# A hybrid layer with top-4-of-32 experts: the phase ahead of the experts written anew, and another order of the last weights

## The chip, the cores and the metric

The kernel runs on one core of one Trainium2 chip. The metric is device time in microseconds (us): 1152.71 us, the median of three runs (1152.39 to 1156.62). One further execution was taken under the profiler; its own time is 1153.48 us.

## The reference

One layer over 256 tokens of 1024 channels, in float32, with 256 context tokens beside them. Biases, norms' gains and the routing by blocks are cut here; `mod` gives six vectors of 1024, from c for the tokens and from c_ctx for the context.

```python
x = x + pos_embed_2d(L)
sh1, sc1, g1, sh2, sc2, g2 = split(silu(c) @ w_mod + b_mod)            # 1024 x 6144
u = rmsnorm(x, norm1_g) * (1 + sc1) + sh1                              # the same for ctx with c_ctx
xa, ga, xb, xc, xd = split(u @ w_in + b_in)                            # 1024 x 1536
ya = (rglru_forward(xa) + rglru_backward(xa)) * gelu(ga)               # 4 causal taps, 2 gates, a scan;
                                                                       # starts from the context's last state
yb = pool_mixer(xb)                                                    # means over 2/4/8/16 positions
yc = fourier_mixer(xc)                                                 # 2-D DFT, real part, linear map
yd = silu(layernorm(conv31(xd[:, :256] * sigmoid(xd[:, 256:])))) @ w_pw
x = x + g1 * (concat(ya, yb, yc, yd) @ w_out + b_out)                  # 1024 x 1024
h = rmsnorm(x, norm2_g) * (1 + sc2) + sh2
top_vals, top_idx = top_k(h @ w_router + b_router, 4); gates = softmax(top_vals)
# each token goes to its 4 experts of 32:
gu = xb @ w_gu[e] + b_gu[e]                                            # 1024 x 2048 per expert
act = (clip(gu[:, 1024:]) + 1) * swish(min(gu[:, :1024], 7))
x = x + g2 * sum(gate * (act @ w_down[e] + b_down[e]))                 # 1024 x 1024 per expert
out = rmsnorm(x, final_norm_g)
```

## The kernel before

All of it is one function, `tile_hybrid_moe`, with a schedule written out by hand: each engine does its instructions in the order of the code, and waits only for data and for buffers. PE is the matrix engine, DVE the VectorE, ACT the ScalarE, POOL the GpSimd, SP the engine that issues the loads. One buffer `B` in SBUF holds everything; its first 18 MB are 18 slots of 1 MB. `bank` is one of eight accumulators of 128 x 512 in PSUM.

**Ahead of the experts** the slots hold the inputs x and ctx, the pieces of `w_mod` and `w_in`, `w_out` and the transposed activations `UT`. PE multiplies silu(c) by `w_mod` in pieces: `gemv_a` (L223) for shift and scale of the first norm, `gemv` 8 to 23 (L250) for the other four vectors. `transposes` turns the normed tokens, `modulate` applies scale and shift to them, `proj` (L309 with 512 columns, L311 with 256) multiplies by `w_in`, one row tile k of 128 at a time and twelve column tiles n. Then come the mixers, their pieces set between one another by hand: `lru_conv` (L424, L426), `lru_gates`, `lru_tanh`, `lru_mid` (L444 to L446), the 31 taps of the conformer convolution for two tiles of channels (62 in all) in `taps_dve` (43 of them on VectorE, L474 to L478) and `taps_act` (19, multiplied on ScalarE and added on GpSimd, L489), closed by `taps_sum` (L492); GpSimd makes the window sums. `scale_out` multiplies rows of `w_out` by g1, `out_mm` (L508) multiplies with the tokens as the weights of PE and 512 columns of `w_out` as what moves, into banks 0 to 3. The vectors that are needed along the free axis are spread over the partitions by GpSimd's `partition_broadcast` (L583, L697, L706, L707 ahead of routing, and L853 to L862 behind it).

`residual` (its add for one half on GpSimd, L772) makes x and its square sums, `norm2` and `hidden` (L785 on GpSimd) the router's input H, `turn` (L793) its transpose, `logits` (L799) the router product, `choose` the top 4, `gates` the softmax. `reseed` (L808) puts x back into the four banks `Y` that collect the result.

**The experts.** An expert's weights are 12 chunks of 1 MB, eight of w_gate_up and four of w_down; all 32 make 402.7 MB. `load_chunk` puts chunk i into slot `RING[i % 18]`, so a chunk can be loaded only when the chunk 18 before it has been multiplied, and the first 18 when the work ahead of the experts has left the slots. All these loads stand in one queue of SP, in the order of the experts. An expert takes at most 64 tokens at once (`CAP`); one with more goes through `block` a second time. For expert e the loop does: `down(e - 1)` (L953), a branch on the count (L1030), `keep` (L980), `gate_up(e)` (L927), `pick` (L904) and `turn_rows` (L912) for the rows of the next expert, `swiglu`, `turn_act` (L945), and the adding of older experts' results to `Y` by `scatter_part` (L984). The last expert's gate and up are cut by four of these, its down runs in two halves of the columns (`down_half`, L966; `keep_half`, L970), and `scatter_half` (L975) adds it in four pieces; the final norm reads the banks `Y`.

## Time and profile before

| | |
|---|---|
| median of three runs | 1152.71 us |
| profiled execution, its own time | 1153.48 us |
| its span (first to last instruction) | 1151.7 us |
| PE busy with matmuls | 1044.3 us, 91% of the span |
| PE busy with loading weights (beside them) | 426.5 us |
| VectorE, ScalarE, GpSimd busy | 307.9, 138.9, 64.6 us |
| DMA over the span | 444.83 MB, 386 GB/s |
| mean granted clock of PE | 0.976 of full speed |

The span is what the trace shows; 1.8 us of the execution lie around it. A share of busy time is a mean over stages that differ, so the rows below are taken stage by stage: ahead of the experts, the expert loop, and the end. In the trace a float32 matmul shows as two instructions, and its count "x" counts both. Some matmul records can be missing.

### The profile page before, as it was taken

The page shows a single profiled execution, that of the slowest core. Times are in us where ns is not written, and L with a number is a line of the kernel's source. Part 1 is how long each engine was busy: PE and PEld are TensorE (multiplying, and loading weights), DVE is VectorE, ACT ScalarE, POOL GpSimd, SP SyncE. Part 2 cuts the span into 40 slices and gives each one's busy share as a digit, 9 for nine tenths or more (in the row PEclk, how much of TensorE's full clock was granted, in tenths as well). Part 3 has the DMA queues.
Part 4 walks back from the last instruction along what each step waited for, and adds up shares of the span by engine and source line. Part 5 has one row for each costly group of instructions (what it writes and reads, how often), then busy time and mean ns, then how long its engine had stood idle before and what let it go on. Part 6 is the DMA issues. An engine that isn't in the chain of part 4 may idle for free. (4 is left out here: it accounts for less than half of the span.)

```text
span 1151.7 us, 12157 instructions
## 1 busy us (share of the span) xinstructions
PE 1044.3 (91%) x4810; PEld 426.5 (37%) x4810; DVE 307.9 (27%) x542; ACT 138.9 (12%) x250; POOL 64.6 (6%) x100
## 2 busy tenths in 40 slices
PE   4998495999999998999999999999889999989996
PEld 2654242333333333333333334444333333333333
DVE  4669494111111211222211111211111111111112
ACT  4335222000000000010000000000000000000002
POOL 2123543000000000000000000000000000000000
PEclk9998798999999999999999999999999999999999
DMA  8977676899999998999999999999999999999993
GB/s 333 376 276 254 238 305 256 334 421 420 420 420 420 421 422 347 422 420 420 421 421 419 421 421 420 419 420 422 420 421 419 421 421 421 420 420 421 421 406 131
DMA packets 68269, 444.83 MB, mean 386 GB/s; under 512 B 7300, under 2 KB 8132, under 8 KB 17448
## 3 DMA queue, kind: packets, MB, share of 16 engines
q1 hardware_dynamic: 67912, 443.36, 94.1%
q8 instruction: 72, 1.18, 0.4%
q14 instruction: 29, 0.24, 0.1%
q0 software_dynamic: 256, 0.05, 0.0%
HBM read 442.34 MB, written 1.05 MB: 385 GB/s over the span
## 5 line engine op out<-in xcount | busy, mean ns | idle before, releaser
L927 PE MATMUL bank<-B 128*64 128x512 f32 x2112 | 475.6, 600 | 12.7 <-DMA B<-in_w_gu_dram 10.9
L927 PEld LDWEIGHTS bank<-B 128*64 128x64 f32 x2112 | 178.8, 138 | 287.8 <-issue 225.7
L953 PE MATMUL bank<-B 128*64 128x512 f32 x1024 | 226.0, 594 | 0.9 <-ACT B L946 0.4
L933 DVE TENSOR_SCALAR B<-bank 128x512 f32<-128x512 f32 x33 | 22.8, 692 | 465.7 <-issue 436.8
L953 PEld LDWEIGHTS bank<-B 128*64 128x64 f32 x1024 | 71.3, 137 | 135.5 <-issue 127.2
L934 ACT ACTIVATE B<-B 128x512 f32<-128x512 f32 x33 | 20.8, 632 | 750.3 <-DVE B L933 750.3
L980 DVE TENSOR_TENSOR B<-bank,B 64x512 f32<-64x512 f32 x64 | 44.1, 689 | 243.6 <-PE bank L953 242.9
L984 PE MATMUL bank<-B 128*128 128x512 f32 x136 | 69.9, 618 | 0.9 <-DVE B L980 0.9
L904 PE MATMUL bank<-B 128*64 128x512 f32 x264 | 66.9, 606 | 1.1 <-DVE B L886 1.1
L916 PE MATMUL bank<-T,E 96*64 96x512 bf16 x196 | 35.6, 395 | 28.4 <-PEq L1030 21.2
L1060 POOL MEMSET B<- 64x1024 f32 x1 | 0.9, 947 | 869.6 <-PE bank L984 869.6
L311 PE MATMUL bank<-B 128*128 128x256 f32 x160 | 38.6, 391 | 0.0
L916 PEld LDWEIGHTS <-E 96*64 96x64 bf16 x196 | 10.9, 106 | 70.3 <-issue 69.3
L904 PEld LDWEIGHTS bank<-B 128*64 128x64 f32 x264 | 22.4, 139 | 36.9 <-issue 33.8
L984 PEld LDWEIGHTS bank<-B 128*128 128x128 f32 x136 | 22.0, 190 | 37.6 <-issue 24.9
L311 PEld LDWEIGHTS bank<-B 128*128 128x128 f32 x160 | 30.2, 193 | 14.2 <-issue 10.6
L913 DVE COPY B<-bank 128x512 f32<-128x512 f32 x33 | 22.8, 692 | 43.8 <-PE bank L912 43.8
L508 PE MATMUL bank<-B 128*128 128x512 f32 x64 | 28.3, 597 | 0.4 <-DVE B L503 0.4
L908 ACT ACTIVATE B<-bank 128x512 f32<-128x512 f32 x33 | 19.7, 597 | 50.7 <-PE bank L904 50.7
L946 ACT ACTIVATE B<-bank 128x512 f32<-128x512 f32 x33 | 19.7, 597 | 48.8 <-PE bank L945 48.8
L912 PEld LDWEIGHTS bank<-B 128*128 128x128 f32 x132 | 16.1, 141 | 22.5 <-ACT B L908 20.6
L478 DVE SCALAR_TENSOR_TENSOR B<-B 128x256 f32<-128x256 f32 x41 | 23.9, 583 | 1.4
(276 smaller groups left out, 581.3 us busy)
## 6 DMA issues: line engine op xcount, KB each, us to landing
B<-in_w_gu_dram SPq DMA_DIRECT2D x256, 1024.0 KB, 19.8
B<-in_w_down_dram SPq DMA_DIRECT2D x127, 1024.0 KB, 19.8
B<-in_w_mod_dram SPq DMA_DIRECT2D x16, 1024.0 KB, 5.1
B<-in_w_mod_dram SPq DMA_DIRECT2D x16, 512.0 KB, 9.9
B<-in_w_in_dram SPq DMA_DIRECT2D x8, 768.0 KB, 13.1
B<-in_w_out_dram SPq DMA_DIRECT2D x4, 1024.0 KB, 6.7
B<-in_ctx_dram SPq DMA_DIRECT2D x1, 1024.0 KB, 5.5
B<-in_x_dram SPq DMA_DIRECT2D x1, 1024.0 KB, 7.6
```

The costliest lines, as they stand in the source:

```text
L311: pe.matmul(half(b, t), w, UT[:, k, 256:512], start=(k == 0 and t == 0), stop=(k == KT - 1 and t == 1))
L478: dve.scalar_tensor_tensor(dst, src, w, dst, op0=ALU.mult, op1=ALU.add)
L508: pe.matmul(bank[2 * c + q], YT[:, k, c * P:(c + 1) * P], w_out_k(k)[:, 512 * q:512 * q + 512], start=first, stop=last)
L904: pe.matmul(mis[0][64 * g:64 * g + 64, :], p[:, c, :], H[:, c, 512 * g:512 * g + 512], start=(c == 0), stop=(c == 1))
L913: dve.tensor_copy(dst, ps.rearrange("p (j n) -> p j n", j=4))
L916: pe.matmul(dst[64 * g:64 * g + 64, :], E3[:, e:e + 1].to_broadcast([96, CAP]), T[:, col:col + 512], start=True, stop=False)
L927: pe.matmul(dst[64 * g:64 * g + 64, :], xt[:, k % 4, (k // 4) * 64:(k // 4) * 64 + 64], w[:, b * 1024 + g * 512:b * 1024 + g * 512 + 512], ...
L933: dve.tensor_scalar(GH, G0, 7.0, 0.5, op0=ALU.min, op1=ALU.mult)
L934: act.activation(TH, GH, AF.Tanh, scale=1.702)
L953: pe.matmul(dst[64 * g:64 * g + 64, :], AT[:, k % 4, (k // 4) * 64:(k // 4) * 64 + 64], dn[e, k, g], start=False, stop=(k == KT - 1))
L980: dve.tensor_tensor(out=dst[p0:p0 + 64, 512 * g:512 * g + 512], in0=ps[64 * g:64 * g + 64, :], in1=G2B[64 * g:64 * g + 64, :], op=ALU.mult)
L984: pe.matmul(Y[c][q], s[:, c * P:(c + 1) * P], o[:, 512 * q:512 * q + 512], start=False, stop=False)
```

## The change

The phase between the loads and the first expert is written anew, and the last two experts' chunks come in another order.

- **Loads and start.** The identity comes as a load (no `make_identity`). `w_in` is loaded in two parts, `W_1` (columns of xa and xd) first and `W_2` later, in place of rows of 6 KB. The biases of the experts are split into three bf16 parts on 128 partitions, and 12 small copies on GpSimd's DMA queue spread them. All four of the first `gemv_a` stand ahead of the turning of x, and `turned_x` applies scale and shift while it empties the bank. The raw x is turned as well, into `XT`.
- **Mixers.** All 62 taps are VectorE's, over four sums. The mixers' order is new: first xa and xd, then xc, xb and ga.
- **Output projection.** `out_mm` has `w_out` as PE's weights and 256 tokens as what moves, so the result comes out transposed; g1 is applied per partition when `finish` adds it to `XT`. The broadcasts of g1, of the bias, of scale and shift ahead of routing go.
- **Routing.** The router multiplies `XT` by rows of `w_router` that were scaled by A2 (`A2c`), a row `LB` holds the bias; the norm's factor comes in behind the product. `natural` turns `XT` back, `seed` puts it into the banks `Y`. H is only scaled by the norm, so `turn_rows`, which runs for every expert, applies A2 and the shift in two VectorE instructions where one copy stood.
- **End.** The chunks come as gate and up of expert 30, gate and up of 31, down of 30, down of 31; `down(30)` stands behind `gate_up(31)`, and expert 30 has its second run, should it need one, in the loop behind the end.

```diff
-W_OUT = [10, 11, 12, 14]
-RING = [4, 0, 1, 2, 3, 13, 15, 8, 5, 6, 7, 9, 10, 11, 14, 12, 16, 17]
+W_OUT = [12, 14, 10, 11]
+RING = [1, 2, 3, 9, 13, 15, 0, 8, 4, 6, 5, 7, 10, 14, 11, 12, 17, 16]
...
+        def load_in1(k):
+            sp.dma_start(W_1[:, k, 0:256], w_in[k * P:(k + 1) * P, 0:256])
+            sp.dma_start(W_1[:, k, 256:768], w_in[k * P:(k + 1) * P, 1024:1536])
+        def load_in2(k):
+            sp.dma_start(W_2[:, k, :], w_in[k * P:(k + 1) * P, 256:1024])
...
+        def turned_x(k):
+            dve.tensor_scalar(UT[:, k, 256:512], half(3 + k // 2, k % 2), A1c[:, k:k + 1], S1c[:, k:k + 1],
+                              op0=ALU.mult, op1=ALU.add)
...
+        for j in range(3):
+            for b in range(4):
+                pool.dma_start(T[32 * j:32 * j + 32, 768 * b:768 * b + 768], BP[32 * b:32 * b + 32, j, :])
...
-        def taps_act(n):
...
-                    act.activation(tp, src, AF.Copy, scale=wdh[:, 2 * j + 1:2 * j + 2])
-                    pool.tensor_tensor(out=ACC[:, 1, :], in0=ACC[:, 1, :], in1=tp, op=ALU.add)
...
+        sums = {(0, 0): ACC[:, 0, :], (1, 0): ACC[:, 1, :], (0, 1): ACC3, (1, 1): ACC2}
+        turns = [(t, j) for j2 in range(0, NTAP, 2) for j in (j2, j2 + 1) if j < NTAP for t in range(2)]
...
+                src, dst, w = V[:, t, j:j + 256], sums[t, j % 2], wdh[:, 2 * j + t:2 * j + t + 1]
...
+                    dve.scalar_tensor_tensor(dst, src, w, dst, op0=ALU.mult, op1=ALU.add)
...
-        def out_mm(k, cs, first=False, last=False):
-            for c in cs:
-                for q in range(2):
-                    pe.matmul(bank[2 * c + q], YT[:, k, c * P:(c + 1) * P], w_out_k(k)[:, 512 * q:512 * q + 512],
-                              start=first, stop=last)
+        def out_mm(k, first=False):
+            for i in range(KT):
+                pe.matmul(half(i // 2, i % 2), w_out_k(k)[:, i * P:(i + 1) * P], YT[:, k, :],
+                          start=(first and i % 2 == 0), stop=False)
...
+        def finish(b):
...
+            for i in (2 * b, 2 * b + 1):
+                dve.scalar_tensor_tensor(XT[:, i, :], half(b, i % 2), G1c[:, i:i + 1], XT[:, i, :],
+                                         op0=ALU.mult, op1=ALU.add)
+        def natural(i):
+            for c in range(2):
+                pe.transpose(N[c][i // 4][:, (i % 4) * P:(i % 4 + 1) * P], XT[:, i, c * P:(c + 1) * P], ident)
+        def seed(c):
+            for i in range(KT):
+                pe.matmul(Y[c][i // 4][:, (i % 4) * P:(i % 4 + 1) * P], XT[:, i, c * P:(c + 1) * P], ident,
+                          start=(i % 4 == 0), stop=False)
+        def logits(k):
+            g = k % 4
+            pe.matmul(bank[0][32 * g:32 * g + 32, 0:256], WRT[:, k, :], XT[:, k, :], start=(k < 4), stop=(k >= 4))
...
+        rsqrt_newton(rs2, w2, tn2)
+        act.activation(SM[:, 1:2], epsc, AF.Exp)
+        for c in range(2):
+            dve.scalar_tensor_tensor(LG[:, c, :], LR[:, c, :], rs2[:, c:c + 1], LB, op0=ALU.mult, op1=ALU.add)
             for q in range(2):
+                act.activation(H[:, c, cols2[q]], N[c][q], AF.Copy, scale=rs2[:, c:c + 1])
...
         def turn_rows(dst, ps):
...
-            dve.tensor_copy(dst, ps.rearrange("p (j n) -> p j n", j=4))
+            dve.tensor_tensor(out=d4, in0=ps.rearrange("p (j g s) -> p j g s", j=4, g=2),
+                              in1=jg(A2c).unsqueeze(3).to_broadcast([P, 4, 2, CAP]), op=ALU.mult)
+            dve.tensor_tensor(out=d4, in0=d4, in1=jg(SH2c).unsqueeze(3).to_broadcast([P, 4, 2, CAP]), op=ALU.add)
...
+        stream = [(e, k) for e in range(NE - 2) for k in range(NCH)]
+        stream += [(e, k) for ks in (range(KT), range(KT, NCH)) for e in (NE - 2, NE - 1) for k in ks]
...
-        gate_up(e, XET, {4: rest[0:2], 5: rest[2:4], 6: rest[4:5]})
-        rest[5]()
+        gate_up(e, XET)
         swiglu()
-        turn_act(e)
+        down(e - 1, mis[1])
+        turn_act(e, AT2)
+        with tc.If(r > CAP):
+            block(e, CAP)
+        keep(OP[1], 0, mis[1])
         down_half(e, 0, range(KT))
         keep_half(0)
         down_half(e, 1, range(4))
+        scatter_part(SS[1], OP[1], 0, 0, 0, 480)
+        scatter_part(SS[1], OP[1], 1, 0, 0, 480)
         down_half(e, 1, range(4, KT))
-        scatter_half(0, ((0, 0, 256), (1, 0, 224)))
         keep_half(1)
```

What the order of instructions on an engine becomes is shown at three places, of before and of the change apart. The first is VectorE between the copy of the first projection (L511 before, L613 now) and the last tap. L424 and L426 (now L481, L483) are the four-tap convolutions, L444 to L446 (now L501 to L503) the middle of a gate, L474 to L478 (now L531 to L535) the 31 taps.

```order
L530 SCALAR_TENSOR_TENSOR B<-B 128x256 x2
L424 TENSOR_SCALAR B<-B 128x512
L426 SCALAR_TENSOR_TENSOR B<-B 128x512 x3
L444 SCALAR_TENSOR_TENSOR B<-B 128x512
L445 SCALAR_TENSOR_TENSOR B<-B 128x512
L446 SCALAR_TENSOR_TENSOR B<-B 128x512
L444 SCALAR_TENSOR_TENSOR B<-B 128x512
L445 SCALAR_TENSOR_TENSOR B<-B 128x512
L446 SCALAR_TENSOR_TENSOR B<-B 128x512
L474 TENSOR_SCALAR B<-B 128x256
L478 SCALAR_TENSOR_TENSOR B<-B 128x256 x7
```

```order
L531 TENSOR_SCALAR B<-B 128x256 x2
L533 TENSOR_SCALAR B<-B 128x256 x2
L535 SCALAR_TENSOR_TENSOR B<-B 128x256 x2
L501 SCALAR_TENSOR_TENSOR B<-B 128x512
L502 SCALAR_TENSOR_TENSOR B<-B 128x512
L503 SCALAR_TENSOR_TENSOR B<-B 128x512
L501 SCALAR_TENSOR_TENSOR B<-B 128x512
L502 SCALAR_TENSOR_TENSOR B<-B 128x512
L503 SCALAR_TENSOR_TENSOR B<-B 128x512
L535 SCALAR_TENSOR_TENSOR B<-B 128x256 x30
L656 TENSOR_TENSOR B<-bank_77,B 128x512
L535 SCALAR_TENSOR_TENSOR B<-B 128x256 x26
```

Six taps now stand ahead of the middles of the first two gates and 56 behind them without another gate between; before, the taps on VectorE come in groups of 8, 10, 13 and 12 with the other gates between.

The second is PE from the last product of the output projection that both have (the residual's banks are 70 to 73 before) to the first expert's bias. L793 turns the router's input before, L808 is the seeding before and `natural` now, L813 `seed`, L799 before and L818 now the router product, L904 and L912 (now L929, L937) pick and turn the first expert's rows; the LDWEIGHTS and their matmuls on UB and OB (the positions of the tokens) are cut at the "...".

```order
L808 MATMUL bank_70<-B 128x512
L808 MATMUL bank_71<-B 128x512
L793 MATMUL bank_74<-B 128x128 x4
L793 MATMUL bank_75<-B 128x128 x4
L799 MATMUL bank_76<-B 32x128 x8
L808 MATMUL bank_72<-B 128x512
L804 MATMUL bank_77<-B 128x32
...
L904 MATMUL bank_76<-B 64x512 x4
L912 MATMUL bank_77<-B 128x128 x4
L1026 TENSOR_LOAD CNT
```

```order
L818 MATMUL bank_70<-B 32x256 x4
L845 MATMUL bank_71<-B 128x32 x2
L813 MATMUL bank_72<-B 128x128 x4
L813 MATMUL bank_73<-B 128x128 x4
L871 LDWEIGHTS UB
...
L929 MATMUL bank_70<-B 64x512 x4
L937 MATMUL bank_71<-B 128x128 x4
L813 MATMUL bank_76<-B 128x128 x4
L813 MATMUL bank_77<-B 128x128 x4
L1055 TENSOR_LOAD CNT
```

The turning of H goes from the way to the router, and half of the seeding stands behind the turning of the first expert's rows.

The third is PE at the end: from the last products of gate and up of the last expert (L927, now L956; bank 75 is the up half's) to the last scattering before the count's branch. L897 turns gated one-hot columns, L953 (now L980) is a whole down product, L966 (now L993) a half one, L945 (now L972) the turning of the activations.

```order
L984 MATMUL bank_72<-B 128x512
L927 MATMUL bank_74<-B 64x512 x2
L927 MATMUL bank_75<-B 64x512 x2
L984 MATMUL bank_73<-B 128x512
L945 MATMUL bank_76<-B 128x128 x4
...
L966 MATMUL bank_77<-B 64x256 x16
...
L966 MATMUL bank_76<-B 64x256 x16
L975 MATMUL bank_70<-B 128x256
L975 MATMUL bank_70<-B 128x224
```

```order
L956 MATMUL bank_75<-B 64x512 x2
...
L980 MATMUL bank_71<-B 64x512 x16
L972 MATMUL bank_70<-B 128x128 x4
...
L993 MATMUL bank_71<-B 64x256 x16
...
L993 MATMUL bank_70<-B 64x256 x8
L1008 MATMUL bank_72<-B 128x480
L1008 MATMUL bank_76<-B 128x480
L993 MATMUL bank_70<-B 64x256 x8
```

The down product of the last expert but one now stands between the last gate and up and the two half products, and two scatterings stand inside the second half.

## Rows read from the trace of the kernel before

**Rows 1.** Windows: stretch, its us, five engines' busy us, clock, DMA, GB/s.
```profile
0.00:202.00 202.00, 151.72 (x706) 81.41 (x708) 132.10 (x263) 68.59 (x120) 63.26 (x97) 0.91 0.77 291
202.00:740.00 538.00, 524.36 (x2423) 203.82 (x2420) 103.75 (x161) 39.65 (x71) 0.00 (x0) 1.00 1.00 412
740.00:1102.00 362.00, 329.02 (x1480) 123.89 (x1478) 62.22 (x96) 23.57 (x42) 1.33 (x3) 0.99 1.01 420
```
The engines stand in the order PE, PEld, DVE, ACT, POOL, each with its instructions; then the granted clock, the DMA engines' busy share and the rate.

**Rows 2.** Windows of 1 us: where the DMA stands, and the last weights.
```profile
205.00:206.00 1.00, 1.00 (x5) 0.36 (x4) 0.00 (x0) 0.00 (x0) 0.00 (x0) 0.57 0.00 0
1133.00:1134.00 1.00, 1.00 (x12) 0.70 (x10) 0.00 (x0) 0.00 (x0) 0.00 (x0) 1.00 0.07 27
```

**Rows 3.** Timeline of PE: the last router product and the first expert matmul.
```profile
190.23 0.92 PE L799 MATMUL bank<-B 128*32 128x128 f32 x16 [0.25 <-ACT B L794]
...
201.91 0.62 PE L927 MATMUL bank<-B 128*64 128x512 f32 x2
```
A row has the start, the busy us, the engine, line and operation, what it writes and reads with the shape, the count, and in brackets the idle time before it with what ended it.

**Rows 4.** Waits of PE: who waits for whom, us, times, longest.
```profile
PE bank L619 <- DVE B L492: 15.5, 1, 15.5
...
PE bank L927 <- DMA B<-in_w_gu_dram: 10.9, 21, 0.6
PE bank L793 <- POOL B L785: 7.6, 1, 7.6
```

**Rows 5.** Timeline of GpSimd: the taps, and the residual's add.
```profile
127.71 6.36 POOL L489 TENSOR_TENSOR B<-B 128x256 f32<-128x256 f32 x8 [11.07 <-issue]
...
181.41 1.08 POOL L772 TENSOR_TENSOR B<-B 128x512 f32<-128x512 f32 x1 [7.85 <-issue]
```

**Rows 6.** Window: the first 23 us.
```profile
0.00:23.00 23.00, 9.36 (x45) 5.71 (x48) 9.74 (x24) 8.60 (x15) 6.24 (x22) 0.93 0.87 312
```

**Rows 7.** Timeline of PE ahead of the experts, one row of each kind.
```profile
28.55 1.93 PE L223 MATMUL bank<-B 128*32 128x256 f32 x32
...
32.65 1.98 PE L309 MATMUL bank<-B 128*128 128x512 f32 x4 [1.17 <-ACT B L242]
...
60.90 7.03 PE L309 MATMUL bank<-B 128*128 128x512 f32 x16
67.76 3.62 PE L311 MATMUL bank<-B 128*128 128x256 f32 x16
...
73.03 1.06 PE L250 MATMUL bank<-B 128*32 128x512 f32 x8
...
89.24 1.05 PE L548 MATMUL bank<-B 128*128 128x128 f32 x8
```

**Rows 8.** Timeline of VectorE: convolution, evictions, gated input, gates, taps.
```profile
68.55 2.33 DVE L426 SCALAR_TENSOR_TENSOR B<-B 128x512 f32<-128x512 f32 x3
...
78.18 0.88 DVE L528 TENSOR_SCALAR B<-bank,B 128x256 f32<-128x256 f32 x2 [1.67 <-PE bank L311]
79.48 0.79 DVE L530 SCALAR_TENSOR_TENSOR B<-B 128x256 f32<-128x256 f32 x2 [0.42 <-ACT B L524]
...
83.01 0.68 DVE L444 SCALAR_TENSOR_TENSOR B<-B 128x512 f32<-128x512 f32 x1
...
88.38 3.96 DVE L478 SCALAR_TENSOR_TENSOR B<-B 128x256 f32<-128x256 f32 x7
```

**Rows 9.** Timeline of the first norm's Newton chain.
```profile
24.12 0.17 DVE L193 TENSOR_SCALAR B<-B 128x2 f32<-128x2 f32 x1 [1.44 <-ACT B L192]
25.55 1.15 ACT L195 ACTIVATE B<-B 128x1024 f32<-128x1024 f32 x1 [1.02 <-DVE B L180]
```

**Rows 10.** Timeline of the end: last expert, its halves, the last scattering.
```profile
1109.93 8.78 PE L927 MATMUL bank<-B 128*64 128x512 f32 x40
...
1131.64 3.67 PE L966 MATMUL bank<-B 128*64 128x256 f32 x32 [0.52 <-ACT B L946]
...
1139.02 0.43 DVE L970 TENSOR_TENSOR B<-bank,B 128x256 f32<-128x256 f32 x1 [3.17 <-PE bank L966]
1141.66 2.41 PE L975 MATMUL bank<-B 128*128 128x32 f32 x12 [0.96 <-PEq L1082]
```

More of the change, by code (lines that the diff above doesn't have):

```diff
@@ new lines, in ln_var, with ln_scale, gemvs @@
+        def ln_var(t):
+            pe.matmul(half(ln_b[t], 0), ONE, hlf(SQ, t), start=True, stop=True)
+            act.activation(hlf(SQ, t), half(ln_b[t], 0), AF.Sqrt, bias=epsc)
+        def ln_scale(t):
+            dve.tensor_tensor(out=hlf(VC, t), in0=hlf(VC, t), in1=hlf(SQ, t), op=ALU.mult)
+            dve.tensor_scalar(hlf(VC, t), hlf(VC, t), lgh[:, t:t + 1], lgh[:, 2 + t:3 + t], op0=ALU.mult, op1=ALU.add)
+        def gemvs(*ks):
+            for i in ks:
+                gemv(i)
+        tiles(XA_, (4, 5, 6, 7))
@@ new lines, in tile_hybrid_moe @@
+        dve.tensor_scalar(xa_view(0), two(bank[0]), bin_(0), None, op0=ALU.add)
+        act.activation(xa_view(1), two(bank[1]), AF.Identity, bias=bin_(1))
+        tiles(DD, (4, 5, 6, 7))
+        load_mod(12)
+        load_out(2)
+        lru_conv((0, 1))
+        lru_gates(0)
+        gemvs(8, 9)
+        for t in range(2):
+            act.activation(VT[:, t, :], half(3, t), AF.Tanh, scale=0.5, bias=hb[:, t:t + 1])
+        lru_tanh(0)
+        for t in range(2):
+            dve.tensor_scalar(V[:, t, 15:271], half(2, t), bin_(8 + t), None, op0=ALU.add)
@@ new lines, in tile_hybrid_moe @@
+        for t in range(2):
+            dve.scalar_tensor_tensor(V[:, t, 15:271], VT[:, t, :], 1.0, V[:, t, 15:271], op0=ALU.add, op1=ALU.mult)
+        lru_gates(1)
+        lru_tanh(1)
+        lru_conv((2, 3))
+        tiles((6, 7), range(8))
+        for t in range(2):
+            act.activation(XC[:, 256 * t:256 * t + 256], half(5, t), AF.Identity, bias=bin_(6 + t))
+        gemvs(10, 11, 12)
+        for t in range(2):
+            for q in range(2):
+                pe.matmul(bank[4][:, 256 * t + 128 * q:256 * t + 128 * q + 128], CS[:, q, :], BD[:, 10 + t, :],
+                          start=(t == 0 and q == 0), stop=(t == 1 and q == 1))
@@ new lines, in tile_hybrid_moe @@
+        lru_gates(3)
+        lru_tanh(3)
+        taps(36)
+        gemvs(13, 14, 15)
+        dve.tensor_tensor(out=MB_, in0=bank[7], in1=MB_, op=ALU.add)
+        for t in range(2):
+            for q, M in enumerate((CL, SL)):
+                for c in range(2):
+                    pe.matmul(half(5, t), Z[:, c, t, 128 * q:128 * q + 128], M[:, c, :],
+                              start=(t == 0 and q == 0 and c == 0), stop=(t == 1 and q == 1 and c == 1))
+        for t in range(2):
+            act.activation(YT[:, 4 + t, :], half(5, t), AF.Identity, bias=v("bf", t))
@@ L753, in tile_hybrid_moe @@
+        Y = [[bank[2], bank[3]], [bank[6], bank[7]]]
         rt = R(O_RT, 572)
@@ L803, in rows_of @@
[L803 to L811 removed]
+        LR = bank[1][:, 0:64].rearrange("p (c e) -> p c e", c=2)
+        CN = bank[1][:, 128:160]
```

834 lines of the change are left out of this document (380 added, 454 removed).

## The prediction

> **What bounds the kernel now.** I read first the busy times of three long stretches [rows 1]. From 202 us on the DMA moves 412 and then 420 GB/s without a break: the experts' weights, 402.7 MB, come in as fast as this kernel ever loads anything. In the first 202 us it moves only 291 GB/s, though PE is busy for 151.7 of them: 202 x (420 - 291) / 420 = 62 us of transfer time are lost there. The reason is in the ring: 18 slots of 1 MB are full before the first expert multiplies, and no weight can be loaded until a slot is given back. The first expert matmul starts at 201.91 us [rows 3]; the DMA still stands at zero between 205 and 206 [rows 2] and runs from then on. At the other end it moves 27 GB/s on average between 1133 and 1134 [rows 2], the last of the weights: I put their landing at 1133.2.
>
> So the time is a sum: T0 (201.9), then 931.3 us of weight stream up to the last landing, then 18.5 us to the end of the span (1151.7), and 1.8 us around it (the profiled execution took 1153.48; the median of the three runs is 1152.71, 0.8 below). Between T0 and the last landing PE was the tighter of the two until about 740 us (524.4 busy of 538) and the DMA after that (PE 329.0 of 362) [rows 1]; in all PE waited only 10.9 us for weights [rows 4]. Both start at T0, so whatever T0 gains, both keep. That makes T0 the first question and the last 18.5 us the second.
>
> **T0, from the start.** The waits of PE [rows 4] name what is lost before T0: 15.5 us for taps that VectorE closes after GpSimd, 7.6 us for a GpSimd add of the router's input. Both stand behind an idle GpSimd: 11.07 us with no releaser before the taps go on, 7.85 us before the add [rows 5], each time just after a partition broadcast and an ISA row in the order. In the new order no broadcast lies ahead of routing, the taps are VectorE's, and no GpSimd work stands between the output projection and T0.
>
> What is left I take as PE's own work, since almost all of it is in one row on that engine. Its start: the first four w_mod tiles, with all that is loaded ahead of them, are 7.0 MB; at the 312 GB/s of the first 23 us [rows 6] they land at 22.4 us. Before, 4.1 us pass from the start of the last products with them (28.55) to the first projection (32.65) [rows 7]. Now VectorE applies scale and shift as it empties four halves of banks (0.44 each, from the 0.88 for two [rows 8]) and 8 transposes follow (0.13 each): 2.8 us more. First projection at 22.4 + 4.1 + 2.8 = 29.3.
>
> From there on, by the pitches of [rows 7] (x counts instructions in the trace, two for one f32 matmul): 48 of 512 columns at 0.44 = 21.1 (32 in the projections, 16 for the gates); 332 of 256 columns at 0.226 = 75.0 (64 + 96 in the projections, 128 in the transposed output projection, 44 in the mixers); 16 adaLN products at 1.06 = 17.0; the second four of the first kind, twice 1.93; the small Fourier product 1.05; 34 transposes at 0.13 = 4.5; the router products twice 0.92, for twice the columns [rows 3]. Sum 124.3. The output projection is no saving: 128 x 0.226 = 28.9 where 64 x 0.44 = 28.1 stood. I add 3 us for short waits in the last stage, where PE and VectorE take turns bank by bank, and get the last router product at 29.3 + 124.3 + 3 = 156.6.
>
> Before, that point is 191.15 (190.23 + 0.92), and T0 follows 10.8 us later [rows 3]. Now the norm is computed beside the router and not before it, so its chain comes after: one more ScalarE pass and the Newton chain (1.43 us from 24.12 to 25.55 [rows 9]), 2.5 in all; 0.4 because both halves of the tokens choose together; and the second seeding of the accumulators, 16 instructions of 128 columns at 0.13 = 2.1, stands on PE between the turning of the first expert's rows and its first matmul. T0 = 156.6 + 10.8 + 2.5 + 0.4 + 2.1 = 172.4, a gain of 29.5 us.
>
> **What has to stay beside it.** VectorE: the projection of the first mixer ends at 56 on PE (29.3 + 14.1, 7.2 for the first half of the fourth mixer's, 3.9 and 1.6 for transposes). Behind it stand in order the copy (0.7), 16 convolution passes (at most 2.33 / 3 = 0.78 each, 12.4), the gated input (0.88 + 0.79), the middle of two gates (6 passes of 0.68, 4.1), 62 taps and their sums (0.8), all by [rows 8], with 1 us of waits. The taps' price is the open one. Before, each tap adds to the result of the one in front: 7 in 3.96 us, 0.566. Two passes of that size that don't depend on each other take 0.79, 0.395. The new taps go round four sums, so I take 0.40: 24.8 us, and VectorE is done at about 101.5. PE comes to the first use (the mean) 49 us behind 56, at 105 (7.2 for the rest of the fourth mixer, 14.4 for two more pairs of column tiles, 7.0 for gates, 13 adaLN products, 6.5 for the Fourier mixer). With 0.566 it would be 35.1 us and 111.8, a wait of 6 to 7 us. The nearest row for a pass without a dependence is the 0.395, so the forecast has no wait; the range keeps both.
>
> [...]
>
> The DMA: 39.2 MB of other inputs and 17 slots of weights must be in by T0, 57.0 MB. The last loads of w_out wait until the last projection has left its slots (117 us by the list above); from there 3 of them and 14 weight tiles, 17.8 MB at 420 GB/s, need 42 us, until about 161. That is 11 us ahead of T0, so the ring is full again but for the slot that holds the residual stream (free with the seeding, less than 2 us before T0), and the weight stream restarts about 4 us behind T0 as before. The twelve small copies that spread the bias tables go out on GpSimd's queue and are needed only by the first expert.
>
> The expert loop: the turning of rows gets a second VectorE pass (about 0.7). PE does not need it before its next gate and up, and a whole down projection lies between. I count it at nothing; without that cover it is 0.7 for each expert, in the half where PE is the tighter (18 experts) 13 us.
>
> **The end.** Before, PE runs gate and up of the last expert from 1109.93 with the scattering of two older experts cut in between, and reaches the down halves at 1131.64, one after the other, 3.67 each, by [rows 10]. Now all gate and up tiles come before the last two downs, so PE does the interleaved work while the down tiles come in. After the last landing there remain half of the second half (1.8), 1 us that PE is behind by then, two evictions at 0.43 (one before), and the 2.2 us from there to the final scattering at 1141.66 with the 10.0 us after it, unchanged: with small gaps 16.2 where 18.5 stood. Gain 2.3. The bounds: 5 if nothing is behind, a loss of 3 if the down of the last but one is.
>
> Sum: 1153.48 - 29.5 - 2.3 = 1121.7 for a profiled execution, 1121 beside the median.
>
> **Rivals.** (1) VectorE is late: taps at 0.566, PE waits 6 us before the means. For it: all the taps that the trace shows ran at that pace; against it: they were dependent. T0 179, time 1127. (2) The DMA is late: it is not the full ring but the loads that decide. For it: loads of w_out stand on one queue ahead of 14 weight tiles. It decides from 11 us of delay on; with 20 us the time is 1130. (3) PE is quicker: no short waits, 0.44 for every pair of 256-column instructions as for one of 512, and the end gains 5. T0 166, time 1112; from 162 on the DMA limits it. (4) Slower: w_in now comes in lines of 1, 2 and 3 KB in place of 6 KB, and PE cannot pass a product whose tile is missing. If the 6.3 MB took 15 + 32 = 47 us, 134 GB/s, all the gain is gone; at 100 GB/s T0 is 221 and the time 1169. Against it: w_mod in 1 KB lines is in the 312 GB/s of the first 23 us. (5) The extra pass of the loop is uncovered: 1134.
>
> **Numbers.** Forecast as summed, 1121, its own range 1115 to 1126: 0.55. Rival (1) 0.17, (2) 0.08, (3) 0.10, (5) 0.05, (4) and the like 0.05. All but the last are faster by over 0.5% (under 1147), which is about what a measurement of this kernel can tell from no change. Faster 0.93, the same 0.03, slower 0.04. Range 1108 to 1136: it leaves out the far ends of (2) and (4) and a quicker PE than (3).
>
> **What would show it.** In the new profile the first expert matmul near 173 us and no PE idle of over 3 us between 30 and 145; VectorE's last tap before PE's mean product; no GpSimd idle row ahead of routing that anyone waits for; DMA at zero for some microseconds just before T0; the stretch from T0 to the last landing still near 931 us; the last landing some 16 us before the end. A first matmul later than 182, or a DMA that never stops before T0, would prove the sum wrong.

## The result and the profile after

The changed kernel takes 1121.12 us (median of 4 runs, 1118.96 to 1123.31) where the kernel before takes 1152.55: ratio 0.9733, 95% interval 0.971 to 0.9755. In a second set of runs it was 1120.24 us, ratio 0.9718 (0.9687 to 0.9749). Forecast were 1121 and a range of 1108 to 1136. The profiled execution took 1123.31 us with a span of 1121.4.

The three long stretches of the changed kernel, cut at its own first expert matmul, in the columns of [rows 1]:

```profile
0.00:172.00 172.00, 149.05 (x798) 100.62 (x799) 107.04 (x277) 59.13 (x111) 34.85 (x77) 0.93 0.89 339
172.00:660.00 488.00, 476.46 (x2214) 182.27 (x2214) 105.80 (x163) 35.70 (x64) 0.00 (x0) 1.00 1.00 412
660.00:1072.00 412.00, 374.71 (x1689) 126.83 (x1688) 81.85 (x124) 27.45 (x49) 0.00 (x0) 1.00 1.01 420
```

The first stretch is 30 us shorter with nearly the same PE work (149.0 us busy in place of 151.7): what went is idle time. Behind it the rates are the 412 and 420 GB/s of before, and GpSimd does nothing at all.

PE's timeline at the points on which the sum was built:

```profile
34.53 1.88 PE L378 MATMUL bank<-B 128*128 128x512 f32 x4
...
60.12 7.07 PE L380 MATMUL bank<-B 128*128 128x256 f32 x32
67.03 1.88 PE L489 MATMUL bank<-B 128*128 128x512 f32 x4
...
101.75 4.50 PE L293 MATMUL bank<-B 128*32 128x512 f32 x40
106.17 1.13 PE L595 MATMUL bank<-B 128*128 128x256 f32 x4
...
157.00 0.64 PE L818 MATMUL bank<-B 128*32 128x256 f32 x8
...
168.10 3.62 PE L813 MATMUL bank<-B 128*128 128x128 f32 x16
172.02 0.62 PE L945 MATMUL bank<-T,E 96*64 96x512 bf16 x4 [0.30 <-PEq L1060]
172.45 13.93 PE L956 MATMUL bank<-B 128*64 128x512 f32 x64
```

The first projection is at 34.53, the means at 106.17 without a wait, the last router product ends at 157.64, the first expert matmul is at 172.45 (201.91 in [rows 3]). VectorE's taps end ahead of the means:

```profile
78.90 11.96 DVE L535 SCALAR_TENSOR_TENSOR B<-B 128x256 f32<-128x256 f32 x30
...
102.22 0.76 DVE L539 TENSOR_TENSOR B<-B 128x256 f32<-128x256 f32 x2
```

The stretches in which the DMA stops, restarts and ends (answering to [rows 2]):

```profile
160.00:163.00 3.00, 1.02 (x11) 0.70 (x10) 2.16 (x15) 2.99 (x6) 0.00 (x0) 1.00 0.83 347
...
166.00:168.00 2.00, 1.31 (x6) 0.81 (x5) 0.00 (x0) 0.60 (x1) 0.00 (x0) 0.50 0.00 0
...
174.00:175.00 1.00, 1.00 (x6) 0.33 (x4) 0.00 (x0) 0.00 (x0) 0.00 (x0) 1.00 0.97 410
...
1104.00:1105.00 1.00, 1.00 (x14) 0.61 (x10) 0.00 (x0) 0.00 (x0) 0.00 (x0) 1.00 0.37 143
1105.00:1106.00 1.00, 1.00 (x6) 0.49 (x3) 0.00 (x0) 0.00 (x0) 0.00 (x0) 1.00 0.06 20
```

The ring is full from about 163 (161 was forecast), and the loads run at their full rate again from 174, 1.5 us behind the first expert matmul, where the prediction had 4. In windows of 0.2 us the DMA falls to nothing at 1105.6; read in the same way, it did so at 1133.6 before, a little behind the 1133.2 of the prediction. From the first expert matmul to there it is 933.1 us (931.7 before), from there to the end 15.8 (18.1 before). So 29.5 us came from the front and 2.3 from the end, and the stream between gave 1.4 back.

### The profile page after: what moved, and what is told of

The parts are those of the page before. It is cut to its first block, busy times and chain, and to the rows that moved or that the text cites. A ratio compares the mean times of both kernels' runs of the same rounds, so it can differ in the third digit from the quotient of the medians.

```text
span 1121.4 us, 12287 instructions
## 1 busy us (share of the span) xinstructions
PE 1036.5 (92%) x4888; PEld 424.1 (38%) x4888; DVE 305.3 (27%) x588; ACT 128.7 (11%) x239; POOL 34.9 (3%) x77
## 5 line engine op out<-in xcount | busy, mean ns | idle before, releaser
L956 PE MATMUL bank<-B 128*64 128x512 f32 x2112 | 473.4, 596 | 35.4 <-DMA B<-in_w_gu_dram 34.1
L956 PEld LDWEIGHTS bank<-B 128*64 128x64 f32 x2112 | 160.4, 137 | 329.1 <-issue 224.2
L980 PE MATMUL bank<-B 128*64 128x512 f32 x1024 | 228.2, 598 | 2.7 <-DMA B<-in_w_down_dram 1.8
L960 DVE TENSOR_SCALAR B<-bank 128x512 f32<-128x512 f32 x33 | 22.8, 692 | 464.3 <-issue 404.0
L980 PEld LDWEIGHTS bank<-B 128*64 128x64 f32 x1024 | 71.6, 138 | 139.7 <-issue 127.6
L1008 PE MATMUL bank<-B 128*128 128x512 f32 (+2 forms) x140 | 69.7, 606 | 3.2 <-PEq L1107 2.3
L929 PE MATMUL bank<-B 128*64 128x512 f32 x264 | 63.4, 599 | 0.9 <-DVE B L866 0.9
L945 PE MATMUL bank<-T,E 96*64 96x512 bf16 x196 | 33.6, 389 | 6.4 <-PEq L1060 4.8
L940 DVE TENSOR_TENSOR B<-bank,B 128x512 f32<-128x512 f32 x33 | 22.8, 692 | 42.7 <-PE bank L937 42.7
L929 PEld LDWEIGHTS bank<-B 128*64 128x64 f32 x264 | 20.4, 137 | 36.6 <-issue 35.6
L945 PEld LDWEIGHTS <-E 96*64 96x64 bf16 x196 | 10.6, 106 | 46.1 <-issue 45.1
L937 PEld LDWEIGHTS bank<-B 128*128 128x128 f32 x132 | 16.5, 143 | 22.4 <-ACT B L933 20.6
L962 DVE TENSOR_SCALAR B<-bank 128x512 f32<-128x512 f32 x33 | 22.8, 692 | 3.7 <-PE bank L956 0.6
L964 DVE SCALAR_TENSOR_TENSOR B<-B 128x512 f32<-128x512 f32 x33 | 22.8, 692 | 3.4
L535 DVE SCALAR_TENSOR_TENSOR B<-B 128x256 f32<-128x256 f32 x58 | 23.2, 481 | 0.0
```

The costliest lines, as they stand in the source:

```text
L535: dve.scalar_tensor_tensor(dst, src, w, dst, op0=ALU.mult, op1=ALU.add)
L929: pe.matmul(mis[0][64 * g:64 * g + 64, :], p[:, c, :], H[:, c, 512 * g:512 * g + 512], start=(c == 0), stop=(c == 1))
L940: dve.tensor_tensor(out=d4, in0=ps.rearrange("p (j g s) -> p j g s", j=4, g=2), in1=jg(A2c).unsqueeze(3).to_broadcast([P, 4, 2, CAP]), op= ...
L945: pe.matmul(dst[64 * g:64 * g + 64, :], E3[:, e:e + 1].to_broadcast([96, CAP]), T[:, col:col + 512], start=True, stop=False)
L956: pe.matmul(dst[64 * g:64 * g + 64, :], xt[:, k % 4, (k // 4) * 64:(k // 4) * 64 + 64], w[:, b * 1024 + g * 512:b * 1024 + g * 512 + 512], ...
L960: dve.tensor_scalar(GH, G0, 7.0, 0.5, op0=ALU.min, op1=ALU.mult)
```

## The experiments

**One part alone: the taps.** The kernel before with all taps on VectorE over four sums:

```diff
-                    act.activation(tp, src, AF.Copy, scale=wdh[:, 2 * j + 1:2 * j + 2])
-                    pool.tensor_tensor(out=ACC[:, 1, :], in0=ACC[:, 1, :], in1=tp, op=ALU.add)
+                src, dst, w = V[:, t, j:j + 256], sums[t, j % 2], wdh[:, 2 * j + t:2 * j + t + 1]
...
+                    dve.scalar_tensor_tensor(dst, src, w, dst, op0=ALU.mult, op1=ALU.add)
```

> The kernel before with one part of the change alone: all 62 taps on VectorE, round four sums; everything else stays. My theory (the wait of 15.5 us at the means was GpSimd's lateness, and independent taps cost 0.40 us): 36 taps behind 105.4 us end at 119.8, the sums at 120.6, PE comes at 119.5, so about 1 us of the 15.5 stays; the first expert matmul moves from 201.9 to about 188 and the time to about 1139. The taps' mean pitch is 0.40. Rival (the idle time of GpSimd behind its broadcast hits the next user): the window sums still start at 127.7, PE waits for the pooling product instead, the gain is 8 us or less, time 1145 or more. Rival (a tap costs its full length whatever it depends on): pitch 0.566, taps end at 126.6, gain 8.

Measured: 1151.44 us, ratio 0.9988 (0.9968 to 1.0007), no gain that can be told from none. In its profile the first expert matmul is at 196.25, 5.7 us earlier and not 14. The taps did what was forecast (36 in 14.33 us, 0.40 each, the wait at the means 3.85 us, where 15.5 stood and 1 was forecast). GpSimd gave it back; its timeline, and VectorE's beside it:

```profile
101.96 16.09 POOL L572 TENSOR_TENSOR B<-B 128x512 f32<-128x512 f32 x1 [38.80 <-ACT B L570]
...
127.76 1.48 POOL L577 PARTITION_BROADCAST B<-B  x2 [7.83 <-issue]
136.54 0.63 POOL L597 TENSOR_TENSOR B<-B 128x271 f32<-128x271 f32 x1 [7.30 <-issue]
```

```profile
102.14 14.33 DVE L479 SCALAR_TENSOR_TENSOR B<-B 128x256 f32<-128x256 f32 x36
116.40 0.74 DVE L486 TENSOR_TENSOR B<-B 128x256 f32<-128x256 f32 x2
```

One GpSimd multiply lasts 16.09 us, from just ahead of the 36 taps to 0.9 us behind the sums. In the kernel before the same multiply took 1.35 us beside the slower taps (13 of them in 8.45 us from 105.41):

```profile
105.04 1.35 POOL L578 TENSOR_TENSOR B<-B 128x512 f32<-128x512 f32 x1 [2.75 <-ACT B L576]
```

So the dense taps shut GpSimd out, and the 7.8 and 7.3 us that it idles around a broadcast come on top; PE waits 7.75 us at the output projection, for rows that wait for that broadcast. The second theory holds in its size; the wait stands at the output projection and not at the pooling product. The Trainium skill, "SBUF — State Buffer", section "SBUF: two separate sides", says that a VectorE instruction with two inputs in SBUF and a GpSimd instruction that reads SBUF lock each other out for a whole instruction. The 16.09 us agree in kind; that the lock holds through 36 instructions in a row, and that the slower, dependent taps let GpSimd in between them, is in the traces alone.

**One part alone: the router's adds.** The kernel before with GpSimd's two adds ahead of the router on VectorE:

```diff
-                eng = pool if (c, q) == (0, 1) else dve
+                eng = dve
...
-                if (c, q) == (0, 1):
-                    act.activation(h, h, AF.Copy, scale=r_)
-                    pool.tensor_tensor(out=h, in0=h, in1=s_, op=ALU.add)
-                else:
-                    dve.scalar_tensor_tensor(h, h, r_, s_, op0=ALU.mult, op1=ALU.add)
+                dve.scalar_tensor_tensor(h, h, r_, s_, op0=ALU.mult, op1=ALU.add)
```

> The kernel before with GpSimd's two adds ahead of the router (one half of the residual, one half of the router's input) on VectorE; everything else stays. My theory: the wait of 7.6 us was for these adds, which stood behind an idle GpSimd; PE then waits 1 us or less there, VectorE has 1.4 us more to do, the first expert matmul comes at 195.5 in place of 201.9 and the time is 1146. Rival (the norm's chain is the next late thing): PE waits 4 us or more for the second half of the tokens, the gain is 3 us or less, time 1150.

Measured: 1147.38 us, ratio 0.9963 (0.9941 to 0.9986), first expert matmul at 194.57. PE at the place of the 7.6 us:

```profile
177.41 1.32 PE L789 MATMUL bank<-B 128*128 128x128 f32 x8 [1.12 <-DVE B L783]
...
180.72 0.91 PE L795 MATMUL bank<-B 128*32 128x128 f32 x16 [1.99 <-ACT B L790]
```

The wait of 7.6 became 1.12, as forecast, and 1.99 for ScalarE; the theory holds. Both parts alone move the first expert matmul by 5.7 and 7.3 us, 13 of the 29.5; by the medians it is 1.5 and 5.5 us of the 31.4. That the rest is what they lack (no broadcast ahead of routing at all, no GpSimd beside the taps) fits, but no run took the broadcasts away alone.

**The old end.** The changed kernel with the chunks in the experts' order and the old last expert:

```diff
-        stream = [(e, k) for e in range(NE - 2) for k in range(NCH)]
-        stream += [(e, k) for ks in (range(KT), range(KT, NCH)) for e in (NE - 2, NE - 1) for k in ks]
+        stream = [(e, k) for e in range(NE) for k in range(NCH)]
...
+        gate_up(e, XET, {4: rest[0:2], 5: rest[2:4], 6: rest[4:5]})
+        rest[5]()
```

> The changed kernel with the old end: chunks in the order of the experts, the last expert's gate and up cut by the four scatterings, down in two halves with the old scattering. My theory: from the last landing to the end 18.5 us in place of 16.4, all before it unchanged, so 2 us more than the changed kernel: 1123. Rival (the new end hides nothing, only its place moved): the same time within 0.5 us, 1121. Rival (the last but one down is late in the new order): the old end is quicker, 1119.

Measured: 1122.07 us, ratio 0.9739 (0.9706 to 0.9772): 1 to 2 us above the changed kernel, less than these runs can tell. The profile tells it. Here the DMA falls to nothing at 1101.2, and the span ends at 1119.5: 18.3 us, where the changed kernel has 15.8.

```profile
1100.00:1101.00 1.00, 1.00 (x14) 0.64 (x12) 0.00 (x0) 0.00 (x0) 0.00 (x0) 1.00 0.28 109
1101.00:1102.00 1.00, 1.00 (x12) 0.70 (x10) 0.00 (x0) 0.36 (x1) 0.00 (x0) 1.00 0.01 2
```

This run has the same front phase, and its first expert matmul stands at 166.62. The first projection was 1.2 us earlier, and the granted clock fell elsewhere. In the changed kernel it fell twice, to 0.56 and 0.59 from 110 to 114, where some 1.7 us were lost, and to 0.50 (1.2 GHz) from 166 to 171, after PE had idled 1.92, 0.86 and 0.69 us for masks, gates and rows; the second half of the seeding (L813) took 3.62 us there. With the old end the clock stayed at 1.00 in both places, and that half took 1.95; it was down from 156 to 159, where PE has to wait anyway. So one profile's first expert matmul can lie some 4.5 us from another's for where the clock falls alone.

**The bias copies.** The first projection was forecast for 29.3 and came at 34.53. The twelve copies were moved twice: by 17 us (from 10.9 to 27.6), and behind 50 us, which is the diff:

```diff
         for j in range(3):
             for b in range(4):
                 pool.dma_start(T[32 * j:32 * j + 32, 768 * b:768 * b + 768], BP[32 * b:32 * b + 32, j, :])
+        sp.dma_start(CS, const[:, 768:1024].rearrange("p (b n) -> p b n", b=2))
+        sp.dma_start(CL[:, 0, :], const[:, 256:512])
+        sp.dma_start(SL[:, 0, :], const[:, 512:768])
         for M in (CL, SL):
```

> The changed kernel with the twelve copies that spread the bias tables issued some 20 us later (behind the modulation of the first half); nothing else. The first projection came at 34.5 us where 29.3 was forecast, because the last of the first w_mod pieces came at 27.9. Theory A (these copies, in flight from 10.9 to some 26 us, slow the loads: 282 to 332 GB/s between 18 and 24 us where the kernel before had 380 to 412): the last piece comes 3 us earlier, the first projection at 31.5 to 32, the first expert matmul at 169.5, time 1118. Theory B (the short lines of w_in, which are issued between the w_mod pieces): no change, first projection 34.5, 1121. Theory C (the copies cost the same wherever they stand): the first projection comes 3 us earlier and the projections then wait 3 us, time 1121.

> The changed kernel with the twelve bias copies issued behind 50 us and the three Fourier tables loaded behind them; no added matmuls. Theory A (the copies cost 4 to 5 us of waiting for w_mod, and nothing else in the run with both edits came from them): first projection at 29, first expert matmul 4 to 5 us ahead of the changed kernel's 170.5 to 172.5, at 166 to 168 with the clock's fall at the same place; the expert loop as in the changed kernel (4.8 us at the branches); time 1116. Theory B (what the start gains, the full ring or the restart takes back): first expert matmul at 167, time 1120 as before.

Measured: moved a little, first projection at 29.20, but 2.3 us of waits for the second w_mod pieces, and the first expert matmul at 168.42; 1120.87 us, ratio 0.9726 (0.9692 to 0.9759), no change that the medians show. Moved far, first projection at 28.68, no such wait, first expert matmul at 166.66 with the clock falling where it fell in the changed kernel; 1116.07 us (1113.76 to 1120.49), ratio 0.9681 (0.9658 to 0.9705). The changed kernel's early loads, then those of this run:

```profile
18.00:21.00 3.00, 1.88 (x27) 0.73 (x25) 2.00 (x8) 1.74 (x5) 1.83 (x4) 0.99 1.05 282
21.00:24.00 3.00, 1.28 (x16) 0.31 (x16) 0.00 (x0) 0.83 (x2) 0.00 (x0) 1.00 1.07 332
```

```profile
18.00:21.00 3.00, 3.00 (x45) 1.44 (x48) 1.60 (x7) 1.91 (x4) 0.00 (x0) 0.79 1.05 388
21.00:24.00 3.00, 1.55 (x28) 0.35 (x21) 0.00 (x0) 0.41 (x1) 0.00 (x0) 1.00 1.06 380
```

With the copies in flight the DMA engines are as busy and move an eighth to a quarter less. The dip goes where the copies go: moved a little, the loads have 379 to 388 GB/s from 18 to 24 and 269 to 333 from 33 to 42. For the near place theory C holds in part: of the 5.3 us at the first projection, 2.3 go into later waits. For the far place theory A holds. This version beats the changed kernel by 4 to 5 us in the medians, with ranges that overlap (1113.76 to 1120.49 and 1117.74 to 1123.31); its profiled execution is the slowest of its five, and there the stream behind the first expert matmul takes 936.1 us, 2 to 3 more than in the changed kernel's two profiles.

**The taps one behind the other.** One sum per tile of channels, each tap adding to the one in front:

```diff
-        sums = {(0, 0): ACC[:, 0, :], (1, 0): ACC[:, 1, :], (0, 1): ACC3, (1, 1): ACC2}
-        turns = [(t, j) for j2 in range(0, NTAP, 2) for j in (j2, j2 + 1) if j < NTAP for t in range(2)]
+        sums = {(t, h): ACC[:, t, :] for t in range(2) for h in range(2)}
+        turns = [(t, j) for t in range(2) for j in range(NTAP)]
```

> The changed kernel with one sum for each tile of channels in place of two, and the 31 taps of one tile behind one another, so that each tap adds to the result of the one in front. Theory A (dependent taps cost 0.566, independent ones 0.397): the taps end at 113 in place of 103, PE waits 7 us for the means, first expert matmul 7 us later, 1128. Theory B (a tap costs the same whatever it depends on): pitch 0.40, no change, 1121. Theory C (the pitch rises, but what stands behind has room: VectorE was idle 3.9 us at 103 and 6.2 us at 111): pitch 0.566, PE waits 7 us, but the first expert matmul is only 2 to 4 us later, 1124.

Measured: 1126.45 us, ratio 0.9767 (0.9725 to 0.9809), first expert matmul at 175.19. VectorE, and PE at the means:

```profile
79.03 12.98 DVE L533 SCALAR_TENSOR_TENSOR B<-B 128x256 f32<-128x256 f32 x25
...
94.94 15.21 DVE L533 SCALAR_TENSOR_TENSOR B<-B 128x256 f32<-128x256 f32 x26
```

```profile
110.31 1.19 PE L592 MATMUL bank<-B 128*128 128x256 f32 x2 [4.27 <-DVE B L533]
```

The 25 dependent taps take 12.91 us to the next instruction, 0.52 each; GpSimd is idle beside them. The 26 take 15.14, 0.58 each, and from 101.6 to 108.2 GpSimd makes its window sums beside them, in 0.6 to 0.9 us a row, so dependent taps do let it in. Over four sums a tap takes 0.40 (26 in 10.29). The dependence alone costs 0.12 us for each tap, then; that the rest of the 0.58 is GpSimd's doing was not tested. Theory B is out. A and C share the higher pitch, and both put the wait too high: it was 4.3 us and not 7, since the taps ended at 110.1 and not at 113. The first expert matmul is 2.7 and 4.7 us behind those of the changed kernel's two profiles, nearer to C.

**Matmuls that should keep the clock up, and a control.** 21 matmuls that nothing reads, on PE where it waits ahead of the first expert; the same with the far copies; and, as a control, 21 shorter ones at 10 us, where PE waits anyway:

```diff
+        fill(bank[0], 12)
         pe.matmul(pos[:, 0, :], UB, MB[:, 0, :], start=True, stop=False)
...
+        fill(bank[0], 5)
         pick(PP[0][:, :, 0, :])
         picked()
+        fill(bank[4], 4)
```

> The changed kernel itself once more, beside the three others of this job. The runs with the same front phase had their first projection at 33.3 and 34.5 us and their first expert matmul at 166.6 and 172.5, so if these are only where the granted clock fell and when the w_mod pieces came, this one lies between: first expert matmul 166 to 173, time 1119 to 1123.

> The changed kernel with 21 more 128-column matmuls on PE, into banks that hold nothing then: 12 ahead of the wait for the one-hot masks, 5 ahead of the first pick, 4 ahead of the turning. Nothing reads them. Theory A (PE's idle 1.9, 0.9 and 0.7 us there let the granted clock fall to 0.5 from 163 to 171, and pick, turning and seeding took 2.71, 1.11 and 3.62 us where the run with the old end had 1.94, 0.66 and 1.95): with PE busy the clock stays at 1.00, 2.9 us less, first expert matmul at 169.5 or earlier, time 1118. Theory B (the clock falls for what PE did long before): the same clock, and the added matmuls delay by up to 1 us.

> The changed kernel with the added PE matmuls of the run before and with the twelve bias copies issued behind 50 us, when the second half of the modulation is done (the three Fourier tables are loaded behind them). Theory A (the copies slow the w_mod pieces only while these are waited for): first projection at 29 to 30, no later wait of PE for loads above what it was (0.6 and 1.4), first expert matmul 4 us earlier than in the run with the added matmuls alone, 165; time 1114. Theory B (the loads are only moved: what does not wait ahead of the projections waits at w_mod pieces 21 and 22 or at w_in): first projection 29 to 30, first expert matmul within 1 us of the other's, time 1118.

> The changed kernel with 21 more matmuls of 32 columns on PE at about 10 us, where PE waits 4 to 6 us for the normed tokens anyway; nothing reads them. As many PE instructions as in the run that kept the clock up, but far from the routing. Theory A (that run lost time because the added instructions shift where the loop's branches and matmuls lie in PE's instruction stream): first expert matmul 170 to 172 as in the changed kernel, the waits at the branches 16 us in place of 4.8, some of over 1 us between 500 and 650, time 1124 to 1126. Theory B (it lost by what it did ahead of the first expert, the banks or the clock): waits at the branches 4.8, time 1120.

Measured: the changed kernel again 1120.24 us, first expert matmul 170.45. With the matmuls in the waits 1125.70, ratio 0.9774 (0.9741 to 0.9806): the clock stays at 1.00 and the first expert matmul is at 167.99, and yet it is 5 us slower in the median. With the far copies too 1121.99 (0.9711 to 0.9775), first projection 28.95, first expert matmul 163.86. The control 1126.81, ratio 0.9772 (0.9745 to 0.9798), first expert matmul 168.43. PE idles 1.92, 0.86 and 0.69 us there as in the changed kernel, and the clock stays at 1.00 all the same, so it is not shown that the added matmuls kept it up. Its second half of the seeding:

```profile
165.75 1.95 PE L816 MATMUL bank<-B 128*128 128x128 f32 x16
```

From the first expert matmul to the end the three take 954.9, 956.1 and 955.5 us, the changed kernel 949.0 and 950.8. Ahead of an expert in the control, then in the changed kernel:

```profile
561.12 0.62 PE L948 MATMUL bank<-T,E 96*64 96x512 bf16 x4 [1.88 <-PEq L1063]
```

```profile
553.88 0.62 PE L945 MATMUL bank<-T,E 96*64 96x512 bf16 x4 [0.16 <-PEq L1060]
```

In the control PE waits 0.8 to 1.9 us at this point for six experts in a row, from 505 to 645, where each costs 0.16 in the changed kernel. All its waits for the branch make 11.1 us (16 was forecast) and 4.8 in the changed kernel. By expert 17 the control is 15.9 us behind, counted from each one's first expert matmul, and by the last expert 5, since it then waits less for weights (25.4 us in place of 34.1). The matmuls at 10 us can hardly touch anything there but the place of the loop in PE's list of instructions: all profiles of the changed kernel and its versions without added PE matmuls have 4.5 to 4.9 us of these waits, the three with them 11.1 to 16.1. Theory A holds. The Trainium skill, "Runtime: NRT & Kernel Launch", section "Instruction fetch mechanics", says that PE's instructions come in blocks of 256 and that a taken branch out of the blocks at hand waits for one. The runs agree as far as they go: they do not show the fetch.

**The extra pass in the loop.** The changed kernel with one copy in place of the two passes, which leaves out scale and shift of the experts' rows, and with four passes more:

```diff
-            dve.tensor_tensor(out=d4, in0=ps.rearrange("p (j g s) -> p j g s", j=4, g=2),
-                              in1=jg(A2c).unsqueeze(3).to_broadcast([P, 4, 2, CAP]), op=ALU.mult)
-            dve.tensor_tensor(out=d4, in0=d4, in1=jg(SH2c).unsqueeze(3).to_broadcast([P, 4, 2, CAP]), op=ALU.add)
+            dve.tensor_copy(dst, ps.rearrange("p (j n) -> p j n", j=4))
```

```diff
+            for _ in range(4):
+                dve.tensor_scalar(dst, dst, 1.0, None, op0=ALU.mult)
```

> The changed kernel with one copy in place of the two VectorE instructions that scale and shift the turned rows of every expert; the experts then work on rows without scale and shift, the routing is as it was. My theory (the second pass is hidden behind a whole down product and, in the second half, behind the weights): no change in the loop, first expert matmul 0.7 us earlier, time 1120. Rival (it is not covered in the half where PE is the tighter): 0.7 us for each of 18 experts, 12 us less, 1108.

> The changed kernel with four more VectorE passes over the turned rows of every expert (each multiplies by 1.0): six where the change has two and the kernel before one. It says how much cover there is. My theory: PE needs the rows only at the next gate and up, 7 us of down product later; the four passes take 2.8 us, and the activations' work on VectorE behind them (two of five passes of the swiglu stand ahead) is delayed by as much at most. No PE wait of more than 1 us for each expert, time 1120 to 1123, the most of it the 2.8 us ahead of the first expert. Rival (the cover is thin): PE waits 2 us or more for each expert in the first half, 40 us more.

Measured: 1117.87 us, ratio 0.969 (0.9664 to 0.9716), and 1129.86, ratio 0.9807 (0.9784 to 0.983). An ordinary expert takes as long with one pass, two or six: from one expert's start to the next 25.88 and 27.13 us with one and with six, 25.89 and 27.12 in the changed kernel. Two experts differ. The one with over 64 tokens turns its second rows with PE waiting. One copy, two passes, six:

```profile
386.50 13.96 PE L954 MATMUL bank<-B 128*64 128x512 f32 x64 [0.30 <-DVE B L940]
```

```profile
391.05 13.95 PE L956 MATMUL bank<-B 128*64 128x512 f32 x64 [1.03 <-DVE B L942]
```

```profile
393.45 15.65 PE L958 MATMUL bank<-B 128*64 128x512 f32 x64 [2.87 <-DVE B L944]
```

The other is the first: only there VectorE makes the gated one-hot columns right behind the turned rows, and PE waits to turn these columns (L922). Again one copy, two passes, six:

```profile
189.18 0.44 PE L922 MATMUL bank<-B 128*128 128x128 f32 x2 [0.64 <-DVE B L917]
```

```profile
191.29 0.44 PE L922 MATMUL bank<-B 128*128 128x128 f32 x2 [1.37 <-DVE B L917]
```

```profile
191.83 0.44 PE L922 MATMUL bank<-B 128*128 128x128 f32 x2 [3.21 <-DVE B L917]
```

The first down product behind this wait takes 8.65 us in the changed kernel, with the granted clock at 0.54 and 0.61 from 192 to 196, and 7.04 with one copy. All ten profiles with two passes or more have it at 8.3 to 8.7, all four with one pass (the kernel before too) at 7.04. From the first expert to the second it is 26.71, 29.11 and 30.97 us.

So the theory holds for 30 experts and misses two: the second pass costs 0.7 us at the one and 2.4 at the first, and the 1117.87 us fit these 3.1. With six passes the two take 3.5 and 1.9 us more than in the changed kernel; the median came 9 us above it and 7 above the top of what I had put, and what of it lies beyond these 5.4 us is open.

## Why the prediction was right, and where it was not

**The mechanism was right.** The gain lies in the time to the first expert matmul, the stream behind it kept its length to some 2 us (931.7 before, 933.1 and 934.4 in the changed kernel's two profiles), and the end gave the forecast 2.3 us. No PE idle of over 3 us is left between 30 and 145, the taps end 3.2 us ahead of the means (3.5 forecast), the ring is full 9 us before the first expert (11 forecast, with 161 where its own terms, 117 and 42, give 159). GpSimd's broadcasts for the experts run from 140 to 145, ahead of the last router product, but nothing on PE waits for them. PE's waits ahead of the first expert matmul sum to 50.1 us before and to 22.9 now. The 15.5 and the 7.6 of [rows 4] are gone, and so is a third that the prediction does not name:

```profile
PE bank L250 <- DVE B L568: 3.9, 1, 3.9
```

Together they are 27.0 of the 29.5 us.

**172.4 forecast, 172.45 measured, by errors that cancel.** That the two agree so closely is luck: the changed kernel's second profile has 170.45. Three terms were off:

| step | forecast | measured |
|---|---|---|
| first projection | 29.3 | 34.53 |
| from there to the last router product's end | 127.3 | 123.1 |
| from there to the first expert matmul | 15.8 | 14.8 |

The start: the twelve copies were costed at nothing because only the first expert needs them. They run beside the w_mod pieces that PE waits for, 5 us. Without them the first projection comes at 28.68, so the rest of that step stood. The PE work: the pitch of 256-column instructions was taken from busy time (16 in 3.62 us), which holds the last one's tail; 32 go in 6.91 us from start to start, 0.216 and not 0.226, and 332 of them make 3.3 us; five adaLN products in a row go in 4.42 us, not 5.3, which is 2.8 for all sixteen. Of these 6.1 us the clock's fall from 110 to 114 took 1.7 back. The routing came 1 us under its term, although the fall of the clock lies in it with nearly 3 us (pick, turning and seeding take 2.71, 1.11 and 3.62 us, in the run with the old end 1.94, 0.66 and 1.95): in the control, where the clock stays at 1.00, it takes 12.0. The term was taken from the kernel before, where the clock was down too (0.65 and 0.50 from 195 to 199, the pick took 3.63 us).

**The rivals.** The first (taps at 0.566) did not come: the taps ran at 0.397. Four sums buy 0.12 to 0.18 us for each tap, as the chain of taps shows. The second did not come, the third only in its pitch. The fourth named the start as the place of a loss, but for the wrong loads: w_in's short lines are in the far-copies run too, and there the start is as forecast. The fifth came at two experts, the first and the one with two runs, for 3.1 us in all and not for 0.7 at each of 18.

**What bounds the stream.** I called PE the tighter until 740. In the changed kernel PE waits for weights from about 660 on, in all

```profile
PE bank L956 <- DMA B<-in_w_gu_dram: 34.1, 59, 1.3
```

against 10.9 us in [rows 4], and the stream is about as long. The kernel before waits at the loop's branches instead, 21.2 us in all, where the changed kernel waits 4.8:

```profile
PE bank L916 <- PEq L1030: 21.2, 30, 2.9
```

So part of the gain could be luck with where the branches came to lie. The traces speak against it. Of the 21.2 us, 18.6 lie behind 700, where a wait at a branch takes the place of a wait for weights. The stream is not longer for them, and at expert 16, ahead of these waits, the kernel before is 461.8 us behind its first expert matmul, the changed kernel 460.6. In the control most of them lie ahead of 645, where PE is the tighter, and there they count: with the added matmuls the stream takes 938 us and more.

## What to carry to other kernels

Sum a front phase from its first wait, and give every transfer that is "only needed later" the price of what it runs beside. A part that is right by itself can be worth nothing until the engine that takes up the next job is free: the taps alone gave 5.7 us of the 29.5, because the faster VectorE shut GpSimd out. A pass that is hidden in an ordinary turn of a loop can still stand open in the first turn. Take pitches from start to start, and compare profiles of the same phase before giving a microsecond a cause.

## What the runs showed of the hardware

- Independent VectorE passes of 128x256 go at 0.40 us, dependent ones at 0.52 by themselves and at 0.58 in a row beside which GpSimd works; 36 independent ones held one GpSimd multiply for 16.09 us, beside dependent ones it took 1.35.
- Twelve copies of 48 KB between places in SBUF, beside large loads, took the loads from 380 to 388 down to 282 to 332 GB/s, and to 269 to 333 at the later place to which they were moved.
- 21 PE matmuls of no use at 10 us, where PE is idle, made a kernel 6 us slower, with waits of 0.8 to 1.9 us at the branches of its loop some 440 to 640 us later.
